# A decoder layer's second-half row norm: ScalarE normalises, weight and bias go onto the transposed banks, GpSimd makes the residual rows

## Chip, cores and metric

The kernel runs on one core of one Trainium2 chip. The metric is the device time of one execution in microseconds (us). Timed runs are given by their median; beside them stands one execution under the profiler, whose trace shows where the time goes.

## What is computed

One layer of a decoder with 1024 tokens and 1024 channels, float32 throughout. A mixer (a convolution group and a sliding-window attention group, one projection in, one out) is followed by a feed-forward network with a short convolution. After each of the two there is a residual with a factor and a LayerNorm over the 1024 channels of a token:

```python
mix = hybrid_mixer(x, ...)
x = layer_norm(DEEPNORM_ALPHA * x + mix, ln1_g[l], ln1_b[l])
ffn = conv_ffn(x, w_up[l], ffn_dw_w[l], ffn_dw_b[l], w_down[l])
x = layer_norm(DEEPNORM_ALPHA * x + ffn, ln2_g[l], ln2_b[l])

def layer_norm(x, g, b):
    mu = jnp.mean(xf, axis=-1, keepdims=True)
    var = jnp.mean(jnp.square(xf - mu), axis=-1, keepdims=True)
    y = (xf - mu) * lax.rsqrt(var + LN_EPS)
    return y * g + b
```

The change concerns the first of these LayerNorms. Its result is used twice: transposed, as input of the feed-forward network, and multiplied by alpha, as the residual of the second LayerNorm.

## The kernel before

The 1024 tokens are worked through as two halves H = 0 and H = 1 of 512 tokens, each of four blocks t of 128 tokens. Every matrix product is done in three passes over high and low parts of both operands (`wh`, `wl` for weights, `xh`, `xl` for activations): ScalarE makes the high part by a cast (L231), GpSimd the low part by a subtraction (L233). Products take 24 matmuls of 128x512: 16 with `wh` (L265, L266), then 8 with `wl` (L268).

The order in which parts of the layer are issued is written out by hand in `SCRIPT`, one letter for one step of a generator: `O` is the output projection of the second half, `s` a set of sums over the first half (`first_sums`), `L` one block of the second half's norm (`second_norm`, which calls `ln1(1, ...)`), `f` a step of the feed-forward network of the first half for its first six channel blocks (`ffn`, with `up_branch`, `up` and `down`). After the script come `last_sum` and the joint stage (`joint`), which works on both halves at once with seven products in place of eight. From the program order and its own simulation of the engines, a scheduler sets the order on each engine's queue. An engine then takes its queue in order. The large products keep their program order (`chain`).

In a block of the norm, `row_stats` (L295) takes the statistics of the 128x1024 rows `a` on VectorE, GpSimd does the inverse root (L293). For both halves the setting `LNM` selects the last branch of `layer_norm_rows`: VectorE subtracts the mean and scales (L311), GpSimd multiplies by the weight row `g` (L312), VectorE adds the bias row `b` (L313). `transpose_split` then transposes the rows in two groups of four 128x128 pieces into two PSUM banks (L278), ScalarE casts each bank to the high part (L281), VectorE subtracts to make the low part (L282). ScalarE multiplies the rows by alpha (L662). For H = 1, `other_sums` goes on in the two banks: it forms the differences between the halves that the joint stage needs (L763 to L773, executed in the helpers at L747 and L750). The second half uses three single banks, `'ln1': 'TCN'`, in turn; bank T also serves `first_sums`. The rows `a` are next read when the joint stage adds its down-projection to them (L720).

The weight and bias rows are loaded once as 128x1024 tiles spread over the partitions, in `first_norm` (`norm1`), and serve both halves. Parameters that are needed as one value for each partition are loaded as rows of 128 by DMAs from ScalarE's queue (L192 to L202) and turned by three transposes (`parameters`, L203), so that `pcol` gives a column.

Of the kernel before, what the change touches and what calls it, by code (L numbers as in the profile page):

```python
# [12 lines left out]
AF = mybir.ActivationFunctionType  # L13
ALU = mybir.AluOpType

P = 128
S = 1024
D = 1024
KT = D // P
# [12 lines left out]
ALPHA = 2.0 ** 0.25  # L32
# [37 lines left out]
def hybrid_layer_kernel(  # L70
# [7 lines left out]
    nc = tc.nc  # L78
# [22 lines left out]
    def psB(shape=(P, 512), tag="T"):  # L101
        return ps.tile(list(shape), F32, name="ps" + tag, tag=tag, bufs=PS[tag])
# [3 lines left out]
    def psk(key, shape=(P, 512)):  # L106
        tags = PT[key]
        k = ps_turn[key] = ps_turn.get(key, -1) + 1
        return psB(shape, tags[k % len(tags)])

    def f(ap):
        return ap.bitcast(F32)
# [27 lines left out]
    def ring(tag, w, n):  # L140
        if tag not in rings:
            rings[tag] = [top[0], 0, n]
            top[0] += w * n
        r = rings[tag]
        o = r[0] + r[1] % r[2] * w
        r[1] += 1
        return tiny[:, o:o + w]
# [6 lines left out]
    def early(o, n, parts=P):  # L154
        return at(56 * 4 * UNIT + 4 * (HC + o), [P, n], F32, "early")[0:parts, :]
# [3 lines left out]
    ident = const[:, 0:P]  # L159
# [16 lines left out]
    def r128(ap):  # L176
        return ap.rearrange("(r c) -> r c", c=P)
# [3 lines left out]
    pr3 = early(3 * P, P)  # L181
# [18 lines left out]
    nc.scalar.dma_start(out=pr1[34:78, :], in_=r128(ffn_dw_b))  # L200
    nc.scalar.dma_start(out=pr1[78:122, :], in_=r128(ffn_dw_w[2]))
    nc.scalar.dma_start(out=pr3[0:88, :], in_=ffn_dw_w[0:2].rearrange("k (r c) -> (k r) c", c=P))  # L202
    def parameters():  # L203
        tp = psB()
        for i, pr in enumerate((pr1, pr2, pr3)):
            nc.tensor.transpose(out=tp[:, i * P:(i + 1) * P], in_=pr, identity=ident)
        nc.vector.tensor_copy(out=par, in_=tp[:, 0:3 * P].rearrange("p (i c) -> p i c", c=P))
        nc.vector.tensor_scalar(out=bq8, in0=par[:, 0, 0:4], scalar1=-0.125, scalar2=None, op0=ALU.mult)

    def pcol(t, i):  # L210
        return par[:, t, i:i + 1]
# [8 lines left out]
    fdb = [pcol(0, 34 + i) for i in range(2 * NC)]  # L220
    fw = [[pcol(2, i) for i in range(2 * NC)], [pcol(2, 44 + i) for i in range(2 * NC)],
          [pcol(0, 78 + i) for i in range(2 * NC)]]

    def cdw(k, c):
        return pcol(1, k * 4 + c)
# [45 lines left out]
    def transpose_split(src, xh, xl, t, key):  # L271
        banks = []
        for q in range(2):
            b = psk(key)
            banks.append(b)
            for k in range(4):
                kt = q * 4 + k
                nc.tensor.transpose(out=b[:, k * P:(k + 1) * P], in_=src[:, kt * P:(kt + 1) * P], identity=ident)  # L278
            bv_ = b.rearrange("p (k t) -> p k t", t=P)
            hd = xh[q][:, :, t * P:(t + 1) * P]  # L280
            nc.scalar.copy(out=hd, in_=bv_)  # L281
            nc.vector.tensor_tensor(out=xl[q][:, :, t * P:(t + 1) * P], in0=bv_, in1=f(hd), op=ALU.subtract)  # L282
        return banks
# [6 lines left out]
    def rsqrt_eps(out_, in_, n, tag="rv"):  # L290
        v = ring(tag, 4, 4)
        nc.vector.tensor_scalar(out=v[:, 0:n], in0=in_, scalar1=EPS, scalar2=None, op0=ALU.add)  # L292
        nc.gpsimd.tensor_tensor(out=out_, in0=v[:, 0:n], in1=mhalf[:, 0:n], op=ALU.pow)  # L293

    def row_stats(r):  # L295
        st = ring("st", 12, 2).rearrange("p (a b) -> p a b", a=2)
        for i in range(2):
            nc.vector.bn_stats(out=st[:, i, :], in_=r[:, i * 512:(i + 1) * 512])
        mv = ring("mv", 2, 2)
        nc.vector.bn_aggr(out=mv, in_=st.rearrange("p a b -> p (a b)"))  # L300
        rstd = ring("rstd", 1, 2)
        rsqrt_eps(rstd, mv[:, 1:2], 1)
        return mv, rstd

    def layer_norm_rows(r, g, b, H):
        mv, rstd = row_stats(r)
        if LNM[H]:
            nc.vector.scalar_tensor_tensor(out=r, in0=r, scalar=mv[:, 0:1], in1=g, op0=ALU.subtract, op1=ALU.mult)
            nc.vector.scalar_tensor_tensor(out=r, in0=r, scalar=rstd, in1=b, op0=ALU.mult, op1=ALU.add)
        else:  # L310
            nc.vector.tensor_scalar(out=r, in0=r, scalar1=mv[:, 0:1], scalar2=rstd, op0=ALU.subtract, op1=ALU.mult)  # L311
            nc.gpsimd.tensor_tensor(out=r, in0=r, in1=g, op=ALU.mult)  # L312
            nc.vector.tensor_tensor(out=r, in0=r, in1=b, op=ALU.add)  # L313
# [12 lines left out]
    def pair(i):  # L326
        return area(2 * i), area(2 * i + 1)
# [326 lines left out]
    def ln1(H, g, b):  # L654
        (h0, l0), (h1, l1) = [pair(i) for i in ((2, 3) if H == 0 else (4, 6))]
        xh, xl = (h0, h1), (l0, l1)
        x1T[H] = (xh, xl)
        for t in range(TB):
            a = acc[H * TB + t]
            layer_norm_rows(a, g, b, H)  # L660
            banks = transpose_split(a, xh, xl, t, "ln%d" % H)
            nc.scalar.mul(out=a, in_=a, mul=ALPHA)  # L662
            if H == 1:
                other_sums(t, *[b.rearrange("p (k t) -> p k t", t=P) for b in banks])
            yield
# [97 lines left out]
    def other_sums(t, b0, b1):  # L763
        (h0, h1), (l0, l1) = [[f(part(a, t)) for a in x_] for x_ in x1T[0]]
        into(b0, b0, h0, ALU.subtract)
        into(b0, b0, l0, ALU.subtract)
        split_to(*[part(a, t) for a in pair(area_of[3])], b0)
        into(b0, h1, b0, ALU.subtract)
        into(b0, b0, l1, ALU.add)
        s2h, s2l = [part(a, t) for a in pair(area_of[2])]  # L770
        split_to(s2h, s2l, b0)
        into(b1, b1, f(s2h), ALU.subtract)
        into(part(last_f, t), b1, f(s2l), ALU.subtract)  # L773
# [207 lines left out]
    norm1 = []  # L981

    def first_norm():
        norm1.extend((bcast_row(ln1_g, 'g1'), bcast_row(ln1_b, 'b1')))
        yield from ln1(0, *norm1)
# [11 lines left out]

    def second_norm():
        lanes.update(LANES_JOINT)
        yield from ln1(1, *norm1)  # L1000

    steps = {'0': glus(0), 'h': line_bias(), 'j': once(lambda: proj_kv(0)), 'i': proj_q(0), 'x': load_x(1),
             'c': conv(0), 'a': attn(0), 'n': conv_norm(0), 'g': glus(1), 'k': once(lambda: proj_kv(1)),
             'q': proj_q(1), 'A': attn(1), 'o': out_proj(0), 'l': first_norm(), 'C': conv(1),
             'N': second_conv_norm(), 'f': ffn(0, alone), 'O': second_out(), 'L': second_norm(),
             's': first_sums()}
    drain(load_x(0))
    parameters()
    for k in SCRIPT:
        if k == 'c':  # L1010
# [63 lines left out]
```

## Time and profile before

| | us |
|---|---|
| median of 3 timed runs | 1112.17 (1111.09 to 1112.24) |
| the profiled execution | 1113.39 |
| its span, first to last instruction | 1111.6 |

| engine | busy us in the span |
|---|---|
| PE (TensorE matmul) | 1050.4 |
| DVE (VectorE) | 788.9 |
| POOL (GpSimd) | 654.5 |
| ACT (ScalarE) | 481.9 |

PE busy is not PE at its peak: matmuls are pipelined, and a row's duration is longer than the step to the next. In steady work a 128x512 matmul starts 0.23 us after the one before it. A row of the trace names the line, the engine, the operation, what is written and read (`out<-in`), shapes and counts. In groups, "busy us, mean ns" are followed by the idle time of the engine just before them and by what ended it. In a row of waits, the three numbers are the total in us, how often, and the longest. In a row of windows, the first numbers are the stretch and its length, then busy time with the number of instructions for PE, PEld (the weight loads), DVE, ACT and POOL, then the granted TensorE clock as a share of full speed, the share of the DMA engines and GB/s.

### The profile page before, as it was taken

The numbers are of one execution on the slowest core, as the hardware profiler recorded it, in microseconds if no ns is written. First come the engines' busy times: TensorE is split into PE (matmuls) and PEld (weight loads), VectorE is DVE, ScalarE is ACT, GpSimd is POOL, SyncE is SP. The second block draws the span as 40 slices with busy tenths as digits, with TensorE's granted clock in tenths as the row PEclk, the third lists the DMA queues.
The fourth block names the chain that finished last, engine by engine and source line by source line (L and its number), as shares of the span: only waits on it lengthen the run. The fifth ranks groups of instructions, "written<-read, shape, count | busy, mean of one in ns | idle before, by whom it ended". The sixth has DMA issues, their size and how long they took to land.

```text
span 1111.6 us, 14383 instructions
## 1 busy us (share of the span) xinstructions
PE 1050.4 (94%) x5113; PEld 873.9 (79%) x5113; DVE 788.9 (71%) x1430; ACT 481.9 (43%) x915; POOL 654.5 (59%) x560
## 2 busy tenths in 40 slices
PE   7999999878968999898999999999999999999996
PEld 5887778778957998676788787878788787888875
DVE  2899789999897448985746656564747566569656
ACT  4546677753548333462515242433425142442430
POOL 3749688775587556455736372746556363636551
PEclk9999999999978999899999999999999999999999
DMA  6535221413600242131211021111212110233321
GB/s 183 160 87 132 77 57 40 139 53 98 186 20 1 78 132 65 50 110 43 76 37 59 20 82 32 58 56 38 76 39 76 35 60 20 76 114 115 113 95 75
DMA packets 115641, 85.19 MB, mean 77 GB/s; under 512 B 20354, under 2 KB 108017, under 8 KB 115569
## 3 DMA queue, kind: packets, MB, share of 16 engines
q1 hardware_dynamic: 112368, 78.92, 23.9%
q10 hardware_dynamic: 3201, 5.35, 1.4%
q8 instruction: 40, 0.66, 0.2%
q14 instruction: 32, 0.26, 0.1%
HBM read 80.05 MB, written 4.21 MB: 76 GB/s over the span
## 4 chain that ended last, share of the span: by engine, by line
PE 76%; DVE 13%; DMA 4%; POOL 3%; ACT 3%; issue 1%; SPq 0%; POOLq 0%; DVEq 0%; ACTq 0%
PE psA L265 6%; PE psA L266 6%; PE psA L268 5%; PE psS L713 2%; PE psS L714 2%; PE psS L715 2%; PE psS L796 2%; PE psS L794 2%; PE psS L793 2%; PE psA L794 2%; PE psA L796 2%; PE psA L793 2%; PE psS L505 2%; PE psA L638 1%; PE psA L713 1%
## 5 line engine op out<-in xcount | busy, mean ns | idle before, releaser
L233 POOL TENSOR_TENSOR wl<-raw,wh 128x512 fp32r<-128x512 f32 x196 | 263.3, 1355 | 162.2 <-ACT wh L231 68.9
L231 ACT CAST wh<-raw 128x512 fp32r<-128x512 f32 x196 | 119.1, 620 | 173.5 <-PE psA L266 24.1
L233 POOL TENSOR_TENSOR wl<-ts,wh 128x512 fp32r<-128x512 f32 x64 | 82.5, 1296 | 155.4 <-ACT wh L231 135.5
L421 DVE SCALAR_TENSOR_TENSOR psC<-hconv,const,psC 128x512 f32<-128x512 f32 x196 | 147.3, 751 | 3.5
L265 PE MATMUL psA<-x,wh 128*128 128x512 f32 x336 | 135.9, 404 | 7.9 <-DVE z L678 4.1
L266 PE MATMUL psA<-x,wh 128*128 128x512 f32 x336 | 134.4, 400 | 0.0
L231 ACT CAST wh<-ts 128x512 fp32r<-128x512 f32 x64 | 39.3, 622 | 177.4 <-PE psS L715 39.2
L268 PE MATMUL psA<-x,wl 128*128 128x512 f32 x336 | 87.2, 396 | 0.6 <-POOL wl L233 0.6
L265 PEld LDWEIGHTS psA<-x,wh 128*128 128x128 f32 x336 | 64.9, 193 | 23.9 <-issue 4.7
L266 PEld LDWEIGHTS psA<-x,wh 128*128 128x128 f32 x336 | 64.9, 193 | 13.5 <-issue 0.2
L268 PEld LDWEIGHTS psA<-x,wl 128*128 128x128 f32 x336 | 62.3, 188 | 15.1 <-issue 1.2
L293 POOL TENSOR_TENSOR tiny<-tiny,const 128x1 f32<-128x1 f32 (+1 forms) x28 | 26.5, 951 | 53.7 <-DVE tiny L292 50.7
L720 DVE TENSOR_TENSOR acc<-psS,acc 128x512 f32<-128x512 f32 x52 | 35.7, 688 | 31.4 <-PE psS L715 31.4
L233 POOL TENSOR_TENSOR ol<-or,oh 128x512 fp32r<-128x512 f32 x32 | 40.7, 1296 | 18.9 <-ACT oh L231 16.6
L793 PE MATMUL psA<-x,wh 128*128 128x512 f32 x112 | 43.6, 389 | 0.0
L794 PE MATMUL psA<-x,wh 128*128 128x512 f32 x112 | 43.6, 389 | 0.0
L793 PE MATMUL psS<-x,wh 128*128 128x512 f32 x112 | 43.6, 389 | 0.0
L794 PE MATMUL psS<-x,wh 128*128 128x512 f32 x112 | 43.6, 389 | 0.0
L832 POOL TENSOR_TENSOR ts<-raw,ts 128x512 f32<-128x512 f32 x32 | 42.0, 1313 | 1.3
L413 POOL TENSOR_TENSOR cp<-cp,cp 128x512 f32<-128x512 f32 x28 | 36.0, 1287 | 8.4 <-ACT cp L409 8.4
L713 PE MATMUL psS<-wh,gh 128*128 128x512 f32 x88 | 35.0, 397 | 5.9 <-ACT gh L693 3.1
L638 PE MATMUL psA<-oh,x 128*128 128x256 f32 x128 | 37.9, 296 | 1.9 <-ACT z L399 1.5
(383 smaller groups left out, 3057.9 us busy)
## 6 DMA issues: line engine op xcount, KB each, us to landing
raw<-in_w_up SPq DMA_DIRECT2D x56, 512.0 KB
raw<-in_w_down SPq DMA_DIRECT2D x28, 512.0 KB
raw<-in_w_in SPq DMA_DIRECT2D x20, 512.0 KB
raw<-in_x SPq DMA_DIRECT2D x8, 512.0 KB
raw<-in_w_in SPq DMA_DIRECT2D x16, 256.0 KB
acc<-in_x SPq DMA_DIRECT2D x8, 512.0 KB
or<-in_w_out SPq DMA_DIRECT2D x64, 64.0 KB
or<-in_w_out SPq DMA_DIRECT2D x8, 512.0 KB
```

What stands on the lines that cost most here:

```text
L231: nc.scalar.copy(out=h, in_=part)
L233: nc.gpsimd.tensor_tensor(out=l, in0=part, in1=f(h), op=ALU.subtract)
L265: m.append(nc.tensor.matmul(out=o, lhsT=wh[kt], rhs=xh[kt], start=kt == 0, stop=False))
L266: m.append(nc.tensor.matmul(out=o, lhsT=wh[kt], rhs=xl[kt], start=False, stop=False))
L268: m.append(nc.tensor.matmul(out=o, lhsT=wl[kt], rhs=xh[kt], start=False, stop=kt == KT - 1))
L421: tap(nc.vector.scalar_tensor_tensor(out=dst if k == KO else total, in0=src, scalar=cdw(k, c), in1=total, op0=ALU.mult, op1=ALU.add))
L638: m.append(nc.tensor.matmul(out=pa[:, 0, :], lhsT=yah[:, c, :], rhs=wa[0][c], start=c == 0, stop=False))
L713: m.append(nc.tensor.matmul(out=o, lhsT=gh[:, tsl], rhs=wh, start=j == 0, stop=False))
L793: m.append(nc.tensor.matmul(out=o, lhsT=wh[k], rhs=xh[k], start=k == 0, stop=False))
L794: m.append(nc.tensor.matmul(out=o, lhsT=wh[k], rhs=xl[k], start=False, stop=False))
L796: m.append(nc.tensor.matmul(out=o, lhsT=wl[k], rhs=xh[k], start=False, stop=k == 3))
L832: nc.gpsimd.tensor_tensor(out=t, in0=x0, in1=x1, op=ALU.subtract)
```

## The change

In the second half, ScalarE applies mean and inverse deviation to the rows in one pass, with the inverse deviation as scale and a new column `shift` (minus mean times inverse deviation, VectorE, 128x1) as bias. The rows are transposed without weight and bias. In the two PSUM banks, ScalarE then applies weight and bias in place, for each of the four 128x128 pieces with one column of each. The copies `l1g` and `l1b` of the parameters for this come from two more DMAs of 8 rows into `pr3`. The cast, the low part and `other_sums` stay. The residual rows are made by GpSimd from the normalised rows by a multiplication and an addition with weight and bias rows that have been multiplied by alpha once (two passes of ScalarE over 128x1024), so that the pass with alpha over the rows goes. The first half is computed as before.

```diff
     nc.scalar.dma_start(out=pr3[0:88, :], in_=ffn_dw_w[0:2].rearrange("k (r c) -> (k r) c", c=P))
+    nc.scalar.dma_start(out=pr3[88:96, :], in_=r128(ln1_g))
+    nc.scalar.dma_start(out=pr3[96:104, :], in_=r128(ln1_b))
...
+    l1g = [pcol(2, 88 + i) for i in range(KT)]
+    l1b = [pcol(2, 96 + i) for i in range(KT)]
...
+    def transpose_norm(src, xh, xl, t, key):
+        banks = []
+        for q in range(2):
+            b = psk(key)
+            banks.append(b)
+            for k in range(4):
+                kt = q * 4 + k
+                nc.tensor.transpose(out=b[:, k * P:(k + 1) * P], in_=src[:, kt * P:(kt + 1) * P], identity=ident)
+            for k in range(4):
+                kt = q * 4 + k
+                col = b[:, k * P:(k + 1) * P]
+                nc.scalar.activation(out=col, in_=col, func=AF.Identity, bias=l1b[kt], scale=l1g[kt])
             bv_ = b.rearrange("p (k t) -> p k t", t=P)
             hd = xh[q][:, :, t * P:(t + 1) * P]
             nc.scalar.copy(out=hd, in_=bv_)
...
-            layer_norm_rows(a, g, b, H)
-            banks = transpose_split(a, xh, xl, t, "ln%d" % H)
-            nc.scalar.mul(out=a, in_=a, mul=ALPHA)
+            if H == 0:
+                layer_norm_rows(a, g, b, H)
+                transpose_split(a, xh, xl, t, "ln0")
+                nc.scalar.mul(out=a, in_=a, mul=ALPHA)
+            else:
+                mv, rstd = row_stats(a)
+                shift = ring("shift1", 1, 2)
+                nc.vector.scalar_tensor_tensor(out=shift, in0=mv[:, 0:1], scalar=-1.0, in1=rstd,
+                                               op0=ALU.mult, op1=ALU.mult)
+                nc.scalar.activation(out=a, in_=a, func=AF.Identity, bias=shift, scale=rstd)
+                banks = transpose_norm(a, xh, xl, t, "ln1")
+                nc.gpsimd.tensor_tensor(out=a, in0=a, in1=g, op=ALU.mult)
+                nc.gpsimd.tensor_tensor(out=a, in0=a, in1=b, op=ALU.add)
             if H == 1:
                 other_sums(t, *[b.rearrange("p (k t) -> p k t", t=P) for b in banks])
...
     def second_norm():
         lanes.update(LANES_JOINT)
+        for row in norm1:
+            nc.scalar.mul(out=row, in_=row, mul=ALPHA)
         yield from ln1(1, *norm1)
```

More of the change, by code (lines that the diff above doesn't have):

```diff
@@ L278, in transpose_split @@
                 nc.tensor.transpose(out=b[:, k * P:(k + 1) * P], in_=src[:, kt * P:(kt + 1) * P], identity=ident)
+            bv_ = b.rearrange("p (k t) -> p k t", t=P)
+            hd = xh[q][:, :, t * P:(t + 1) * P]
+            nc.scalar.copy(out=hd, in_=bv_)
+            nc.vector.tensor_tensor(out=xl[q][:, :, t * P:(t + 1) * P], in0=bv_, in1=f(hd), op=ALU.subtract)
+        return banks
+    def transpose_norm(src, xh, xl, t, key):
[10 more added lines that the diff above has]
+                nc.scalar.activation(out=col, in_=col, func=AF.Identity, bias=l1b[kt], scale=l1g[kt])
             bv_ = b.rearrange("p (k t) -> p k t", t=P)
```

## The prediction

> **What bounds the kernel now.** I read the page first, for the busy shares of the engines, then the table of windows around the changed stage, then what the matmuls waited for there, and last the rows of VectorE (DVE), ScalarE (ACT) and GpSimd (POOL) in it.
>
> ```profile
> PE 1050.4 (94%) x5113; PEld 873.9 (79%) x5113; DVE 788.9 (71%) x1430; ACT 481.9 (43%) x915; POOL 654.5 (59%) x560
> ...
> 420.00:500.00 80.00, 74.33 (x363) 61.42 (x363) 76.01 (x122) 37.03 (x63) 45.97 (x31) 0.96 0.24 71
> 510.00:1000.00 490.00, 481.15 (x2113) 395.72 (x2112) 296.62 (x498) 182.99 (x309) 265.39 (x208) 1.00 0.18 56
> ```
>
> TensorE is busy for 94% of the span, so the time can only fall where TensorE loses time. From 510 to 1000 us it loses 8.9 us in 490 (490 - 481.15), with a granted clock of 1.00: what an earlier start of that stage gains is kept to the end. The second half's norm runs between about 422 and 495 us. There VectorE is busy for 76.0 of 80 us (95%), ScalarE for 37.0 (46%) and GpSimd for 46.0 (57%). In this stage VectorE, not TensorE, is the full engine.
>
> What TensorE loses there is in the next rows: the waits of the matmuls between 410 and 520 us, then three stretches of 10 us (the last three numbers of a row are the granted clock, the DMA share and GB/s).
>
> ```profile
> PE psA L265 <- DVE z L678: 4.1, 2, 3.5
> PE psS L713 <- ACT gh L693: 3.1, 1, 3.1
> PE psA L265 <- ACT wh L231: 0.7, 1, 0.7
> PE psA L268 <- POOL wl L233: 0.6, 1, 0.6
> PE psS L715 <- DVE gl L694: 0.2, 1, 0.2
> ...
> 450.00:460.00 10.00, 6.26 (x26) 4.59 (x25) 10.00 (x12) 5.69 (x10) 7.20 (x4) 0.90 0.36 105
> 460.00:470.00 10.00, 10.00 (x40) 8.06 (x39) 9.61 (x18) 3.67 (x7) 0.00 (x0) 0.76 0.01 2
> 500.00:510.00 10.00, 6.88 (x23) 5.16 (x22) 6.83 (x10) 2.64 (x5) 5.86 (x4) 0.83 0.07 20
> ```
>
> The waits sum to 8.7 us (4.1 + 3.1 + 0.7 + 0.6 + 0.2). After each of the two long ones the clock drops: 0.76 in the ten microseconds after the wait of 3.5 us, which costs 0.24 x 10 = 2.4 us, and 0.83 around the wait of 3.1 us, which costs 0.17 x 10 = 1.7 us. So the stage loses 12.8 us in all, and this is the most that the change can win here. The first stall, 3.5 + 2.4 = 5.9 us, ends with VectorE's L678, the last step of the up-projection's convolution. The second, 3.1 + 1.7 = 4.8 us, ends with ScalarE's L693.
>
> **What VectorE no longer does.** The next rows are the groups of VectorE and GpSimd in the stage, and single rows of the time line.
>
> ```profile
> L313 DVE TENSOR_TENSOR acc<-acc,bo 128x1024 f32<-128x1024 f32 x4 | 6.3, 1581 | 0.0
> L311 DVE TENSOR_SCALAR acc<-acc,tiny 128x1024 f32<-128x1024 f32 x4 | 5.0, 1272 | 0.0
> L691 DVE TENSOR_TENSOR z<-z,z 128x512 f32<-128x512 f32 x3 | 4.3, 1450 | 0.1
> L694 DVE TENSOR_TENSOR gl<-z,gh 128x512 fp32r<-128x512 f32 x4 | 4.1, 1020 | 0.7 <-ACT gh L693 0.7
> L691 DVE TENSOR_TENSOR z<-z,sq 128x512 f32<-128x512 f32 x1 | 1.6, 1582 | 0.0
> L292 DVE TENSOR_SCALAR tiny<-tiny 128x1 f32<-128x1 f32 x4 | 0.6, 146 | 0.0
> L312 POOL TENSOR_TENSOR acc<-acc,g 128x1024 f32<-128x1024 f32 x4 | 10.4, 2600 | 2.4 <-DVE acc L311 2.4
> ...
> 447.37 2.53 DVE L691 TENSOR_TENSOR z<-z,z 128x512 f32<-128x512 f32 x1
> 449.82 2.31 DVE L313 TENSOR_TENSOR acc<-acc,bo 128x1024 f32<-128x1024 f32 x1
> 452.05 1.78 DVE L694 TENSOR_TENSOR gl<-z,gh 128x512 fp32r<-128x512 f32 x1
> 458.39 0.73 DVE L678 SCALAR_TENSOR_TENSOR z<-psA,const,z 128x510 f32<-128x510 f32 x1
> 464.61 0.68 DVE L691 TENSOR_TENSOR z<-z,z 128x512 f32<-128x512 f32 x1
> 444.17 5.18 POOL L312 TENSOR_TENSOR acc<-acc,g 128x1024 f32<-128x1024 f32 x2
> ```
>
> Removed: four L311 (5.0 us) and four L313 (6.3 us), 11.3 us of VectorE's time. All eight lie ahead of the L678 at 458.39 that ends the first stall. Added: four `shift` operations on 128x1; the nearest row is L292 with 0.146 us, so 0.6 us at most.
>
> The same rows show that VectorE and GpSimd hinder one another. L691 takes 0.68 us alone (464.61, where the window row has GpSimd at 0.00) and 2.53 us at 447.37, beside the two L312 that end at 449.35. The four L691 and four L694 together take 4.3 + 1.6 + 4.1 = 10.0 us in place of 8 x 0.68 = 5.4, an excess of 4.6 us at a GpSimd share of 57%. The change doubles the row operations on GpSimd: eight of 2.60 us in place of four, 10.4 us more, a share of 70% (56.4 of 80). By proportion the excess grows to 4.6 x 70/57 = 5.6 us, so 1.0 more. The bounds are zero, if the new operations fall where VectorE has no operation on two SBUF inputs, and 8 x 2.60 = 20.8, if each holds one up for its whole length. I take 1.0. VectorE's balance is 11.3 - 0.6 - 1.0 = 9.7 us.
>
> The Trainium skill says in "SBUF — State Buffer", "Who interferes with whom", that a VectorE instruction with two SBUF inputs and a GpSimd instruction that reads SBUF exclude one another, and that the one which starts first holds the shared pair for its whole length. The 2.53 us of L691 agree. By that rule the doubled GpSimd work speaks against the change, and it is a rival below.
>
> **What this relief is worth.** L678 at 458.39 is late only because the queue ahead of it is full; with 9.7 us less in that queue, more than the 3.5 us that TensorE waited, the first stall should go with its slow clock: 5.9 us. The second stall is another case. It is the tail behind the last row block: ScalarE's casts of the last sum stand in its queue ahead of the last up-projection's bias (L673), and TensorE has nothing left in order but what needs L693.
>
> ```profile
> 497.99 1.65 ACT L750 CAST x<-lastf 128x512 fp32r<-128x512 f32 x3
> 499.55 0.78 ACT L673 ACTIVATE z<-psA,const 128x512 f32<-128x512 f32 x1
> 504.17 0.62 ACT L693 CAST gh<-z 128x512 fp32r<-128x512 f32 x1 [2.66 <-DVE z L691]
> ```
>
> An earlier start moves these three together, so I leave the 4.8 us in, and I leave the 1.5 us of short waits.
>
> **What ScalarE takes over.** The rows are the groups of the scale that goes, of the bank's cast, of the bias with two column operands, and a four-way scaling of 128x128 out of PSUM from the attention.
>
> ```profile
> L662 ACT ACTIVATE acc<-acc 128x1024 f32<-128x1024 f32 x4 | 4.3, 1068 | 0.0
> L281 ACT CAST x<-psC 128x512 fp32r<-128x512 f32 x3 | 1.8, 589 | 0.3 <-PE psC L278 0.3
> L673 ACT ACTIVATE z<-psA,const 128x512 f32<-128x512 f32 x7 | 5.5, 779 | 2.8 <-PE psA L268 2.8
> ...
> L565 ACT ACTIVATE x<-psY,const x32: 345/367/387, 159.8 to 369.8; 128x128 fp32r<-128x128 f32 x32
> ```
>
> Two column operands cost 779 - 589 = 190 ns over a plain pass. The row norm is then L662 plus that, 1.26 us, and it takes the place of L662 (1.07): four times 0.19 = 0.8 us more. Thirty-two operations on 128x128 go into the banks: 0.37 each by L565, which has one column operand, 0.46 with half of the 190 ns on top; I take 0.37, so 11.8 us (14.7 at the upper end). No row shows one of them writing PSUM in place; below, the start-to-start step of L565 would be less than its 0.37, and I allow 0.29, so 9.3. Scaling the two rows of weight and bias by alpha is two of L662, 2.1 us. In all 14.7 us more, 51.7 of 80: ScalarE still has room. It lies beside TensorE, except that a bank is held 4 x 0.37 = 1.5 us longer before its cast. Against this stands the path ahead of the transposes: L311, L312 and L313 (1.27 + 2.60 + 1.58 = 5.5 us) are replaced by a shift and one ScalarE pass (0.15 + 1.26 = 1.4), so a block is 4.1 us earlier before its two banks cost it up to 3.0. I count this pair at nothing; if the transposes do not move up, the cost of the bank steps is open, up to 4 x 3.0 = 12 us.
>
> **What GpSimd takes over.** The multiply moves behind the transposes and an add follows it: a pair of 2 x 2.60 = 5.2 us per block. The rows that it makes are first needed in the joint stage, long after. But its queue is in order, and the low halves of the weights (L233) stand in it, for which the last eight of the 24 matmuls of an up-projection wait.
>
> ```profile
> L233 POOL TENSOR_TENSOR wl<-raw,wh 128x512 fp32r<-128x512 f32 x23 | 34.2, 1513 | 30.5 <-PE psS L714 16.2 <-PE psA L268 6.1 <-PE psY L715 4.5
> ...
> 495.15 1.81 PE psA L268 x8
> ```
>
> Sixteen matmuls run first, 2 x 1.81 = 3.6 us of cover. One pair ahead of a needed split costs 5.2 - 3.6 = 1.6 us; GpSimd's idle 30.5 us around these splits hides most pairs. I count one: 1.6 us.
>
> **The start.** Two more DMAs of 8 rows are issued from ScalarE's queue.
>
> ```profile
> 12.09 0.30 ACTq L202 DMA_DIRECT2D early<-in_ffn_dw_w  x1
> 12.84 0.58 ACT L281 CAST x<-psT 128x512 fp32r<-128x512 f32 x1 [0.52 <-DMA early<-in_ffn_dw_w]
> 14.98 0.62 ACT L231 CAST wh<-raw 128x512 fp32r<-128x512 f32 x1 [1.56 <-DMA raw<-in_w_in]
> ```
>
> At 0.30 us each they delay the cast at 12.84 by 0.6, and the 1.56 us of idle before the next ScalarE work hide that. Without this cover it costs 0.6 us.
>
> **The sum.** -5.9 + 1.6 = -4.3 us. The profiled execution took 1113.39 us (span 1111.6), 1.22 above the median of the three timed runs, 1112.17. On the profiled execution's scale that is 1109.1, on the median's 1107.9, and I forecast the latter.
>
> **The rivals.** *Both stalls go.* If the last block's transposes come up by more than the 4.1 us, the last sum is done before L673 needs ScalarE, and nearly all of the 12.8 us goes: 1112.17 - 11 = 1101. For it speaks VectorE's 95%, against it the in-order tail above. *GpSimd holds VectorE up.* If each of the eight row operations meets one two-input operation of VectorE and holds it for half its length, that is 8 x 1.3 = 10.4 us against the 11.3 removed; the first stall stays and the time is 1112. The Trainium skill's rule named above ("SBUF — State Buffer") is this mechanism. *The banks take the place of the rows.* The three PSUM banks of this norm are reused by the four blocks; with 1.5 us more per bank on three uses in turn, 4.5 us cancel the 4.3, and the time is 1112 again. *Slower: GpSimd becomes the gate.* If the pairs of two blocks stand together ahead of a needed split, TensorE waits 10.4 - 3.6 = 6.8 us and pays a slow clock of 2.4 behind it: +9.2 against -5.9, so 1115.5, and up to 1118 where a single pair also lands badly. It decides from the point at which over 5.9 + 3.6 = 9.5 us of row work is ahead of one split. For it speaks that GpSimd, with 70%, becomes the second fullest engine; against it, its idle stretch from 457 to 473 us. *The change moves other work.* The order on each engine is made by a scheduler that simulates the whole program, so that the two DMAs and the new operations can reorder work elsewhere, or the pass be placed so late that nothing is relieved. The short waits in the stage (0.6 and 0.7 us) say what a few such shifts cost: within 3 us either way.
>
> **How the numbers follow.** Chances: forecast 0.40 (1103 to 1109.9); both stalls go 0.12; GpSimd holds VectorE up 0.08; the banks 0.11; GpSimd as the gate 0.21; other work moved 0.08, of which 0.02 faster, 0.02 same, 0.04 slower. About 0.2%, 2.2 us, is what a measurement of this kernel can tell from no change. Faster is 0.40 + 0.12 + 0.02 = 0.54, same 0.08 + 0.11 + 0.02 = 0.21, slower 0.21 + 0.04 = 0.25. The range goes from 1100 (most of the 12.8 us) to 1117 (the slower rival without its worst end). The forecast's own range is 1103 to 1109.9.
>
> **What would show it.** Right: the wait of L265 for L678 is gone and the clock at 460 to 470 us is near 1.00, VectorE has about 10 us less in the stage, and the joint stage's first product starts 4 to 5 us earlier. Wrong: L691 and L694 with a mean above 1.4 us (GpSimd holds VectorE), waits of L268 for L233 of several microseconds (GpSimd as the gate), waits of the transposes or of ScalarE's bank steps that end late (the banks), or a difference that stands already before 420 us (other work moved).

## The result and the profile after

| | before | after |
|---|---|---|
| median of 4 timed runs, us | 1112.2 (1111.09 to 1112.52) | 1106.2 (1104.47 to 1107.02) |
| the profiled execution, us | 1113.39 | 1105.66 |
| its span, us | 1111.6 | 1103.9 |

The four of before are the three timed runs shown above and one more. The ratio on record is 0.9939, with a 95% interval of 0.9922 to 0.9956; the two medians alone divide to 0.9946, which lies inside it. They differ by 6.0 us, where 4.3 were forecast. The profile of after is read in the same order as that of before. Lines of the code have moved: the matmuls of the large products are now L270, L271 and L273, ScalarE's cast of the weights L236, GpSimd's low part L238, the up-projection's bias L706, its convolution's last step L711, `gh` L726, `gl` L727, and the down-projection L746 to L748. First the page's busy times of the engines:

```profile
PE 1047.1 (95%) x5113; PEld 872.3 (79%) x5113; DVE 780.9 (71%) x1426; ACT 496.3 (45%) x949; POOL 660.6 (60%) x564
```

Over the whole span VectorE has 8.0 us less (788.9 before), ScalarE 14.4 more (481.9) and GpSimd 6.1 more (654.5). Next the windows view of after, over the stretches that were shown of before (busy times of PE, PEld, DVE, ACT and POOL, then granted clock, DMA share, GB/s):

```profile
420.00:500.00 80.00, 73.54 (x359) 60.76 (x359) 68.90 (x120) 51.59 (x97) 54.94 (x37) 0.99 0.24 73
450.00:460.00 10.00, 9.35 (x46) 7.47 (x45) 9.96 (x17) 5.92 (x14) 4.15 (x3) 1.00 0.20 58
460.00:470.00 10.00, 8.87 (x40) 6.80 (x39) 9.41 (x17) 6.41 (x13) 8.82 (x5) 1.00 0.18 54
490.00:500.00 10.00, 6.73 (x27) 5.19 (x26) 7.35 (x9) 4.80 (x9) 7.15 (x6) 0.93 0.18 52
500.00:510.00 10.00, 10.00 (x42) 8.14 (x41) 4.87 (x8) 1.78 (x3) 3.10 (x3) 0.90 0.00 0
```

The clock between 450 and 470 us is 1.00, where it was 0.90 and 0.76. It still falls around 500 us (0.93, then 0.90). What the matmuls of after waited for between 410 and 520 us (total, how often, longest) says why:

```profile
PE psS L746 <- ACT gh L726: 3.9, 2, 3.3
PE psA L270 <- ACT wh L236: 1.4, 1, 1.4
PE psA L273 <- POOL wl L238: 0.8, 1, 0.8
PE psS L829 <- POOL wl L238: 0.5, 1, 0.5
PE psS L748 <- DVE gl L727: 0.3, 1, 0.3
```

The first stall, the wait for the up-projection's convolution, is gone from the list. The second, for `gh`, stands there with 3.3 us. The wait of 0.5 us at L829 belongs to the joint stage (it ends at 513.34). Before has the same one at its own L796, 0.5 us, but at 520.68 and so just outside its list. Without it the rows of after sum to 6.4 us, against 8.7 before: the waits give 2.3. The 4.1 us for the convolution are gone, and longer waits for `gh` (0.8 more), `wh` (0.7), `wl` (0.2) and `gl` (0.1) have taken 1.8 back. The rest is the clock, in one window over the stage, first of before and then of after:

```profile
420.00:510.00 90.00, 81.20 (x384) 66.57 (x384) 82.84 (x131) 39.66 (x67) 51.83 (x35) 0.94 0.22 66
```

```profile
420.00:510.00 90.00, 83.54 (x399) 68.90 (x399) 73.77 (x128) 53.37 (x100) 58.04 (x40) 0.98 0.22 65
```

A clock of 0.98 in place of 0.94 over 90 us is 3.6 us. With the 2.3 us of waits that makes 5.9. This is an estimate: a clock rounded to hundredths leaves each of the two open by 0.45 us. To compare runs, a stage with ends of its own serves better than fixed times: from the last matmul of the second half's output projection to the first product of the joint stage's down-projection into bank A. These two marks are the last and the first start time in two rows of the trace by line, here for before and then for after:

```profile
L644 PE MATMUL psA<-oh,x x128: 278/283/283, 223.5 to 428.8; 128*128 128x256 f32 x128
L713 PE MATMUL psA<-wh,gh x64: 387/389/496, 553.0 to 1008.3; 128*128 128x512 f32 x64
```

```profile
L667 PE MATMUL psA<-oh,x x128: 277/283/283, 221.0 to 426.6; 128*128 128x256 f32 x128
L746 PE MATMUL psA<-wh,gh x64: 389/389/496, 545.7 to 1000.5; 128*128 128x512 f32 x64
```

The stage takes 553.0 - 428.8 = 124.2 us before and 545.7 - 426.6 = 119.1 after: 5.1 less. Of the 7.7 us between the two spans, 2.2 stood already at the stage's start (428.8 and 426.6), and the joint stage gives the last 0.5 (455.3 us from first to last product, then 454.8). The 2.2 us go back to the first 25 us, before anything of this change but its two DMAs: the first product into bank S starts at 24.1 us in before and at 21.5 in after. In the time line, the products ahead of it follow at steps of 0.43 us in before (16.24, 16.67) and of 0.24 us in after (15.90, 16.14): TensorE's slow steps at the start last longer in the one execution than in the other. Whether the change does this is asked below (e4 and e5).

### The profile page after: what moved, and what is told of

Same layout as the page of the kernel before. It is cut to its first block, busy times and chain, and to the rows that moved or that the text cites. A ratio compares the mean times of both kernels' runs of the same rounds, so it can differ in the third digit from the quotient of the medians.

```text
span 1103.9 us, 14411 instructions
## 1 busy us (share of the span) xinstructions
PE 1047.1 (95%) x5113; PEld 872.3 (79%) x5113; DVE 780.9 (71%) x1426; ACT 496.3 (45%) x949; POOL 660.6 (60%) x564
## 4 chain that ended last, share of the span: by engine, by line
PE 77%; DVE 11%; POOL 4%; DMA 3%; ACT 3%; issue 1%; SPq 0%; POOLq 0%; ACTq 0%; DVEq 0%
PE psA L270 6%; PE psA L271 6%; PE psA L273 6%; PE psS L746 2%; PE psS L748 2%; PE psS L747 2%; PE psS L829 2%; PE psA L829 2%; PE psA L827 2%; PE psS L827 2%; PE psA L826 2%; PE psS L826 2%; PE psS L528 2%; DVE psC L444 1%; PE psA L661 1%
## 5 line engine op out<-in xcount | busy, mean ns | idle before, releaser
L238 POOL TENSOR_TENSOR wl<-raw,wh 128x512 fp32r<-128x512 f32 x196 | 260.1, 1339 | 139.0 <-ACT wh L236 67.4
L236 ACT CAST wh<-raw 128x512 fp32r<-128x512 f32 x196 | 119.2, 619 | 168.3 <-PE psA L271 19.9
L238 POOL TENSOR_TENSOR wl<-ts,wh 128x512 fp32r<-128x512 f32 x64 | 82.5, 1296 | 155.1 <-ACT wh L236 135.3
L270 PE MATMUL psA<-x,wh 128*128 128x512 f32 x336 | 132.7, 395 | 4.4 <-ACT wh L236 3.5
L271 PE MATMUL psA<-x,wh 128*128 128x512 f32 x336 | 132.0, 393 | 1.4 <-DVE x L287 1.4
L236 ACT CAST wh<-ts 128x512 fp32r<-128x512 f32 x64 | 39.4, 622 | 177.4 <-PE psS L748 39.2
L273 PE MATMUL psA<-x,wl 128*128 128x512 f32 x336 | 87.2, 395 | 0.8 <-POOL wl L238 0.8
L270 PEld LDWEIGHTS psA<-x,wh 128*128 128x128 f32 x336 | 63.1, 188 | 19.1 <-ACT wh L236 4.1
L271 PEld LDWEIGHTS psA<-x,wh 128*128 128x128 f32 x336 | 63.1, 188 | 14.6 <-DVE x L287 1.7
L273 PEld LDWEIGHTS psA<-x,wl 128*128 128x128 f32 x336 | 62.4, 188 | 15.3 <-POOL wl L238 1.2
L238 POOL TENSOR_TENSOR ol<-or,oh 128x512 fp32r<-128x512 f32 x32 | 40.7, 1292 | 17.3 <-ACT oh L236 17.3
L826 PE MATMUL psA<-x,wh 128*128 128x512 f32 x112 | 43.6, 389 | 0.0
L827 PE MATMUL psA<-x,wh 128*128 128x512 f32 x112 | 43.6, 389 | 0.0
L865 POOL TENSOR_TENSOR ts<-raw,ts 128x512 f32<-128x512 f32 x32 | 41.9, 1310 | 1.3
L746 PE MATMUL psS<-wh,gh 128*128 128x512 f32 x88 | 34.9, 397 | 6.3 <-ACT gh L726 3.9
```

The lines of the kernel that those rows point to most:

```text
L236: nc.scalar.copy(out=h, in_=part)
L238: nc.gpsimd.tensor_tensor(out=l, in0=part, in1=f(h), op=ALU.subtract)
L270: m.append(nc.tensor.matmul(out=o, lhsT=wh[kt], rhs=xh[kt], start=kt == 0, stop=False))
L271: m.append(nc.tensor.matmul(out=o, lhsT=wh[kt], rhs=xl[kt], start=False, stop=False))
L273: m.append(nc.tensor.matmul(out=o, lhsT=wl[kt], rhs=xh[kt], start=False, stop=kt == KT - 1))
L746: m.append(nc.tensor.matmul(out=o, lhsT=gh[:, tsl], rhs=wh, start=j == 0, stop=False))
```

## Experiments

All of them are read by the same stage. The table has its length, VectorE's busy time in it from the windows view, the median of the timed runs, and the ratio to before of the same set with its 95% interval.

| run | stage, us | DVE busy, us | median, us | ratio |
|---|---|---|---|---|
| before | 124.2 | 99.4 | | |
| after | 119.1 | 89.6 | 1106.2 | 0.9939 [0.9922, 0.9956] |
| e1, rows on VectorE | 125.4 | 97.2 | 1114.47 | 1.0015 [0.9999, 1.0032] |
| e2, norm on VectorE | 118.8 | 90.5 | 1108.88 | 0.9972 [0.9958, 0.9986] |
| e3, ScalarE norm alone | 123.3 | 99.0 | 1112.32 | 1.0004 [0.9991, 1.0016] |
| e4, two DMAs alone | 123.8 | 100.3 | 1112.03 | 1.0013 [0.9995, 1.0031] |
| e5, after again | 118.9 | 89.3 | 1107.47 | 0.9952 [0.9935, 0.9970] |
| e6, last casts on VectorE | 122.1 | 92.7 | 1109.77 | 0.9969 [0.9953, 0.9985] |
| e7, bank steps out | 119.9 | 88.9 | 1108.37 | 0.9958 [0.9939, 0.9977] |
| e8, row steps out | 120.4 | 87.0 | 1109.93 | 0.9969 [0.9952, 0.9986] |
| e9, tail in order | 116.4 | 89.8 | 1102.64 | 0.9904 [0.9878, 0.9930] |
| e10, row steps halved | 120.3 | 87.6 | 1108.01 | 0.9958 [0.9940, 0.9976] |
| e11, e9 again | 114.2 | 88.3 | 1102.99 | 0.9915 [0.9895, 0.9935] |
| e12, e9 and e10 | 115.4 | 86.0 | 1104.07 | 0.9927 [0.9903, 0.9950] |

One program twice gives the noise of a single trace: after and e5 differ by 0.2 us in the stage, e9 and e11 by 2.2. Differences of a stage length below about 2 us decide nothing here.

### Is it VectorE's relief, or the shorter path?

The theory of the prediction (A in the expectations) is that VectorE's queue was full and has less in it now. Its rival (B) is that the path from the statistics to the transposes is shorter. The windows of VectorE ahead of the first stall speak for A. Here are the stretches from 430 to 450 us of before, then of after:

```profile
430.00:440.00 10.00, 10.00 (x47) 8.23 (x46) 10.00 (x20) 3.93 (x7) 7.52 (x7) 1.00 0.14 52
440.00:450.00 10.00, 9.35 (x48) 7.67 (x47) 9.96 (x11) 3.25 (x7) 10.00 (x7) 1.00 0.18 52
```

```profile
430.00:440.00 10.00, 10.00 (x52) 8.38 (x51) 6.40 (x17) 9.70 (x17) 6.24 (x6) 1.00 0.15 53
440.00:450.00 10.00, 10.00 (x46) 8.28 (x45) 9.28 (x12) 7.47 (x16) 8.82 (x6) 1.00 0.36 100
```

In before VectorE is busy for 10.00, 9.96 and 10.00 us of the three stretches from 430 to 460, so it did not stand waiting for rows or banks ahead of the late L678 at 458.39. In after it has 6.40 and 9.28 in the first two, and the L711 in its place starts at 450.04.

e1 keeps the path of after and puts the row operations on VectorE, behind the transposes:

```diff
-                nc.gpsimd.tensor_tensor(out=a, in0=a, in1=g, op=ALU.mult)
-                nc.gpsimd.tensor_tensor(out=a, in0=a, in1=b, op=ALU.add)
+                nc.vector.tensor_tensor(out=a, in0=a, in1=g, op=ALU.mult)
+                nc.vector.tensor_tensor(out=a, in0=a, in1=b, op=ALU.add)
```

> As the changed kernel, but the residual rows are made by VectorE (two 128x1024 operations per block, 4 x 2 x about 1.2 us = 9.6 us) and not by GpSimd. Theory A (the gain is VectorE's relief): the 9.7 us are taken back, the first stall returns, 1109 to 1113 us. Rival B (the gain is the shorter path ahead of the transposes, whatever VectorE carries): the path is the same as in the changed kernel, 1105 to 1107 us. Rival C (the gain comes from the start, by the two new DMAs): 1105 to 1107 as well.

The groups of e1 (busy us, mean ns, then idle time before them) have the 12.0 us that went back:

```profile
L694 DVE TENSOR_TENSOR acc<-acc,g 128x1024 f32<-128x1024 f32 x4 | 6.0, 1503 | 3.0 <-PE psT L297 3.0
L695 DVE TENSOR_TENSOR acc<-acc,bo 128x1024 f32<-128x1024 f32 x4 | 6.0, 1492 | 0.0
```

The whole gain is gone: a stage of 125.4 us and a ratio of 1.0015, although mean, deviation, weight and bias are still applied by ScalarE, as in after. The median of 1114.47 lies just above A's range and far above B's. A had expected the first stall itself to return, and it did not: no product into bank A waits for the convolution, and the clock from 460 to 470 us is 1.00. Only two of the eight row operations stand ahead of that step (L711 at 453.10). The loss comes later, where the other six are. These are waits of e1 between 410 and 520 us that neither before nor after has:

```profile
PE psT L297 <- issue: 2.3, 1, 2.3
PE psY L746 <- DVE z L711: 1.7, 1, 1.7
PE psY L746 <- DVE acc L753: 1.1, 1, 1.1
```

Two of them end with VectorE by name. The first has no releaser in the profile; its transposes into bank T start at 472.41, 0.1 us after VectorE's last read of that bank (L780, 471.64 to 472.31), so VectorE is its likely cause. The cleanest pair is e1 and e8 (below), which has no row operations on any engine: with the path of after in both, VectorE's 12.0 us lengthen the stage from 120.4 to 125.4 us, and the intervals of the two ratios are apart. So the short path alone gives nothing when VectorE is full, which is A against B. That the relief would do without the shorter path is not shown; e3 was meant to test it.

e2 puts one part back, the row norm, as a single operation of VectorE in place of the shift and of ScalarE's pass. GpSimd keeps both row operations.

```diff
-                shift = ring("shift1", 1, 2)
-                nc.vector.scalar_tensor_tensor(out=shift, in0=mv[:, 0:1], scalar=-1.0, in1=rstd, ...)
-                nc.scalar.activation(out=a, in_=a, func=AF.Identity, bias=shift, scale=rstd)
+                nc.vector.tensor_scalar(out=a, in0=a, scalar1=mv[:, 0:1], scalar2=rstd, op0=ALU.subtract, op1=ALU.mult)
```

> As the changed kernel, but the row norm is VectorE's tensor_scalar of before (L311) in place of shift and ScalarE's pass. Theory A: VectorE gets back 4 x 0.8 to 1.25 us = 3.2 to 5.0 of the 9.7 it was relieved of; what is left, 5 to 6 us, still covers the wait of 3.5, so 1106 to 1109. Rival B: the path ahead of the transposes stays short (no L312, no L313), 1105 to 1107. If ScalarE's pass is what counts: 1110 to 1113.

The stage is 118.8 us: it holds the whole gain without ScalarE's row norm, the step that the change's title begins with. The median of 1108.88 lies in A's range. In the groups of e2 that operation costs less than it did before, 3.2 us for four (5.0 before):

```profile
L689 DVE TENSOR_SCALAR acc<-acc,tiny 128x1024 f32<-128x1024 f32 x4 | 3.2, 802 | 0.0
```

VectorE's total is only 0.9 us above that of after, for its eight two-input operations of the up-projection take 7.9 us here (11.1 in after). What relieves VectorE enough is thus the bias row, which went to GpSimd, together with an order that lets the norm run faster. The timed ratio of e2 is the weaker of the two (0.9972, after 0.9939 and 0.9952). Its profile is 0.9 us longer than that of e5 behind the stage (a span of 1106.8 less 548.1, where e5 has 1105.8 less 548.0). Where that comes from stays open.

e3 is the other half: ScalarE normalises, and all else is as before, with the bias row on VectorE ahead of the transposes and no work in the banks.

```diff
                 nc.scalar.activation(out=a, in_=a, func=AF.Identity, bias=shift, scale=rstd)
-                banks = transpose_norm(a, xh, xl, t, "ln1")
                 nc.gpsimd.tensor_tensor(out=a, in0=a, in1=g, op=ALU.mult)
-                nc.gpsimd.tensor_tensor(out=a, in0=a, in1=b, op=ALU.add)
+                nc.vector.tensor_tensor(out=a, in0=a, in1=b, op=ALU.add)
+                banks = transpose_split(a, xh, xl, t, "ln1")
+                nc.scalar.mul(out=a, in_=a, mul=ALPHA)
...
-        for row in norm1:
-            nc.scalar.mul(out=row, in_=row, mul=ALPHA)
```

> As the changed kernel in the row norm (ScalarE), but weight and bias on the rows ahead of the transposes as before (GpSimd multiplies, VectorE adds), the banks as before, ScalarE's pass with alpha back. Theory A: VectorE is relieved of 5.0 - 0.6 = 4.4 us, just over the wait of 3.5, so part of the gain, 1107 to 1110. Rival B: the path still holds L312 and L313 and gains nothing, 1111 to 1113.

No gain (1.0004), though 5.0 us of L311 were to go for 0.6 us of shifts. The windows row says that VectorE was not relieved at all (99.0 us, before 99.4), and the groups of e3 say why:

```profile
L694 DVE TENSOR_TENSOR acc<-acc,bo 128x1024 f32<-128x1024 f32 x4 | 7.4, 1852 | 0.0
L690 DVE SCALAR_TENSOR_TENSOR tiny<-tiny 128x1 f32<-128x1 f32 x4 | 3.9, 973 | 0.4 <-POOL tiny L316 0.4
```

7.4 + 3.9 = 11.3 us, by chance just the 5.0 + 6.3 that the two operations of before took. The shift works on one number for each partition, and its four take 0.97 us in the mean. The time line of e3 shows the longest of them inside an operation of GpSimd:

```profile
440.70 3.15 POOL L693 TENSOR_TENSOR acc<-acc,g 128x1024 f32<-128x1024 f32 x1
441.51 2.36 DVE L690 SCALAR_TENSOR_TENSOR tiny<-tiny 128x1 f32<-128x1 f32 x1
```

Both end at about 443.86 us. An operation planned at 0.15 us took as long as the rest of the GpSimd operation beside it. In after, where the row operations of GpSimd follow the transposes, all four shifts run alone (the trace of after by line: shortest, median and longest in ns):

```profile
L690 DVE SCALAR_TENSOR_TENSOR tiny<-tiny x4: 149/154/160, 425.0 to 434.9; 128x1 f32<-128x1 f32 x4
```

So A's forecast of 1107 to 1110 failed because the relief failed, and B's of 1111 to 1113 came true. e3 fits A's count as measured (no relief, no gain), but it can't tell A from B: it has neither the relief nor the short path.

### What the added work costs

e4 is before with the two DMAs of the start alone, and e5 is after once more.

```diff
+    nc.scalar.dma_start(out=pr3[88:96, :], in_=r128(ln1_g))
+    nc.scalar.dma_start(out=pr3[96:104, :], in_=r128(ln1_b))
```

> The kernel before with the two DMAs of 8 rows and nothing else (the columns are not used). Theories A and B: no change, 1111 to 1113 us. Rival C (the 2.5 us by which the changed kernel's profile is ahead at 24 us come from the DMAs at the start): 1109 to 1110, with the first products at the full clock in its profile.

> The changed kernel once more, as the measure for the other runs of this set. 1105 to 1108 us. Its first profile had its first products at the full clock and was 2.5 us ahead at 24 us; if that is the phase of the clock and not the change, this profile may begin slow and be ahead by about 5 us only, all of it between 428 and 500 us.

e4 doesn't move the time (1.0013 [0.9995, 1.0031]). In e5 the same program as after starts its first product into bank S at 23.1 us, not at 21.5, and keeps the stage of 118.9. Its stage starts at 429.1 us, where that of before starts at 428.8. So the DMAs give and cost nothing that can be measured, and the 2.2 us by which the profile of after is ahead at the stage belong to the execution.

e7 and e8 leave out one added cost each: the thirty-two steps of ScalarE in the banks, and the eight row operations of GpSimd.

```diff
-            for k in range(4):
-                kt = q * 4 + k
-                col = b[:, k * P:(k + 1) * P]
-                nc.scalar.activation(out=col, in_=col, func=AF.Identity, bias=l1b[kt], scale=l1g[kt])
```

> The changed kernel without the 32 operations that apply weight and bias in the banks; the feed-forward input of the second half lacks weight and bias. If these 14 us of ScalarE lie beside other work and their delay of the banks is paid by the shorter path, as the prediction counts: within 1 us of the changed kernel. If the banks are what is late now: 2 to 5 us faster.

```diff
-                nc.gpsimd.tensor_tensor(out=a, in0=a, in1=g, op=ALU.mult)
-                nc.gpsimd.tensor_tensor(out=a, in0=a, in1=b, op=ALU.add)
```

> The changed kernel without the eight row operations on GpSimd; the residual rows of the second half lack weight, bias and alpha. The prediction's price for them is 1.6 us (GpSimd's queue) plus some of the 1.0 us by which VectorE is held up: 1.5 to 3 us faster than the changed kernel. If GpSimd is the gate now: 4 us or more. If they are hidden: no change within 1 us.

Neither is faster than e5 of the same set (1108.37 and 1109.93 against 1107.47). e8 was expected within 1 us or faster and came out 2.5 us slower, though its interval overlaps that of e5. So no cost of either can be measured. The price of 1.6 us for GpSimd's queue isn't there: the longest wait for the low parts is 0.6 us in e8 and 0.8 in after. But leaving out work also changes the order, and what e8 saves there it loses at ScalarE's cast of the weights, for which one wait is 2.5 us long (1.4 in after).

### What ends the second stall

The prediction put the second stall down to ScalarE's queue: the casts of the last sum stand ahead of the last up-projection's bias. e6 moves those casts to VectorE.

```diff
-            split_to(*[x_[k] for x_ in sums[4]], last_f[:, k, :])
+            h, l = [x_[k] for x_ in sums[4]]
+            nc.vector.tensor_copy(out=h, in_=last_f[:, k, :])
+            into(l, last_f[:, k, :], f(h), ALU.subtract)
```

> The changed kernel, with the four casts of the last sum (the high parts in last_sum) on VectorE and not on ScalarE. If the second stall is ScalarE's queue ahead of the last up-projection's bias, as the prediction says: the bias comes up to 2.2 us earlier (the four casts take 2.17 us in the changed kernel) and the time is 1.5 to 3 us under the changed kernel's. Rival (VectorE's queue ends the stall): no change within 1 us.

Neither came true: the time is 2.3 us above that of e5, and the stall got longer. In the waits of e6 between 410 and 520 us it is 4.8 us,

```profile
PE psS L746 <- ACT gh L726: 5.4, 2, 4.8
```

and its time line shows what the convolution stood behind:

```profile
494.22 1.53 DVE L813 CAST x<-lastf 128x512 fp32r<-128x512 f32 x3
...
496.60 1.88 DVE L780 TENSOR_TENSOR x<-lastf,x 128x512 fp32r<-128x512 f32 x3
498.48 0.73 DVE L709 SCALAR_TENSOR_TENSOR z<-psA,const,z 128x511 f32<-128x511 f32 x1
```

L709 is a step of the last up-projection's convolution, and it starts where the last sum's work on VectorE ends. The time line of after has the last sum ahead on both engines, so that clearing one queue could not do:

```profile
489.64 2.17 ACT L783 CAST x<-lastf 128x512 fp32r<-128x512 f32 x4
490.28 3.36 DVE L780 TENSOR_TENSOR x<-lastf,x 128x512 fp32r<-128x512 f32 x4 [1.27 <-ACT x L783]
491.71 0.77 ACT L706 ACTIVATE z<-psA,const 128x512 f32<-128x512 f32 x1
493.63 0.73 DVE L709 SCALAR_TENSOR_TENSOR z<-psA,const,z 128x511 f32<-128x511 f32 x1
...
496.85 0.62 ACT L726 CAST gh<-z 128x512 fp32r<-128x512 f32 x1 [2.80 <-DVE z L724]
```

L706 starts when the casts are done, and L709 waits 1.15 us more (492.48 to 493.63) for the subtractions. e9 therefore orders both, the casts behind the last up-projection's `gh` and the subtractions behind its `gl`. Nothing else of after changes.

```diff
+            up_end[0] = (nc.scalar.copy(out=gh, in_=zu),
+                         nc.vector.tensor_tensor(out=gl, in0=zu, in1=f(gh), op=ALU.subtract))
...
+            i = nc.scalar.copy(out=h, in_=last_f[:, k, :])
+            j = nc.vector.tensor_tensor(out=l, in0=last_f[:, k, :], in1=f(h), op=ALU.subtract)
+            for o, before in zip((i, j), up_end[0]):
+                tc.add_manual_dep(o.ins, before.ins.name, order, reason="the last up-projection first")
```

> The changed kernel, with the casts and subtractions of the last sum ordered behind the last up-projection's gate (its gh on ScalarE, its gl on VectorE). In the run with the casts on VectorE the last L709 stood behind them there, so the second stall is taken to end with both queues. If so, gh comes about 3 us earlier, the stall of 3.3 us and its slow clock of 1.7 go, and the time is 2 to 4 us under the changed kernel's. Rival (the joint stage's second product needs the last sum's buffers, by way of GpSimd's ts, and waits as long): no change within 1 us, the wait only moves to the products.

> The kernel with the last sum behind the last up-projection, once more: its first set had six runs only. If the second stall was worth what its profile shows (2.7 us between the second half's output projection and the first joint down-projection), 1103 to 1106 us, a ratio of 0.991 to 0.995; if the first set's 0.9904 was in part the phase of the clock at the start, the upper end of that.

The time line of e9 has the casts of the last sum (now L815) behind `gh` (L728):

```profile
494.82 0.62 ACT L728 CAST gh<-z 128x512 fp32r<-128x512 f32 x1 [2.45 <-DVE z L726]
495.34 2.18 ACT L815 CAST x<-lastf 128x512 fp32r<-128x512 f32 x4
```

Measured from the start of the stage, `gh` comes 1.8 us earlier than in after (68.42 us in place of 70.25), not 3. About half of it is the queue of VectorE: L709 starts at 66.1 in place of 67.0. The other half is the product of the two branches ahead of `gh` (`z<-z,sq`), which takes 0.69 us in place of 1.58: in after GpSimd's L865 runs beside it, which needs the last sum and now comes later.

The longest wait for `gh` goes from 3.3 to 1.2 us in e9 and to 0.6 in e11, whose longest waits between 410 and 520 us are these (the one at L832, for ScalarE's cast of the weights, is new):

```profile
PE psA L270 <- ACT wh L236: 1.4, 1, 1.4
PE psT L832 <- ACT wh L236: 0.9, 1, 0.9
PE psA L273 <- POOL wl L238: 0.8, 1, 0.8
PE psS L748 <- ACT gh L728: 0.6, 1, 0.6
```

The windows row of e11 over its stage has a clock of 1.00:

```profile
429.00:543.20 114.20, 110.14 (x497) 90.01 (x496) 88.25 (x148) 68.21 (x127) 84.70 (x61) 1.00 0.24 74
```

At 1102.64 and 1102.99 us, with ratios of 0.9904 and 0.9915, this version beats both kernels: some 4 us on top of the change, against the 5.0 that the prediction's count gives for the second stall in after (3.3 and a slow clock of 1.7). After and e9 were timed in different sets, and the ends of their intervals touch (0.9922 to 0.9956 and 0.9878 to 0.9930). Within e9's own set, e10, which is after with halved row steps and has after's tail, is 5.4 us slower than e9, and these intervals are apart.

### Shorter operations on GpSimd

The last question is the contention: do half as long operations on GpSimd hinder VectorE less, and does that shorten the stage? e10 halves them, and e12 is e10 with the order of e9.

```diff
-                nc.gpsimd.tensor_tensor(out=a, in0=a, in1=g, op=ALU.mult)
-                nc.gpsimd.tensor_tensor(out=a, in0=a, in1=b, op=ALU.add)
+                for c in (slice(0, 512), slice(512, D)):
+                    nc.gpsimd.tensor_tensor(out=a[:, c], in0=a[:, c], in1=g[:, c], op=ALU.mult)
+                    nc.gpsimd.tensor_tensor(out=a[:, c], in0=a[:, c], in1=b[:, c], op=ALU.add)
```

> The changed kernel, with each of the eight row operations on GpSimd split in two of 128x512. If VectorE's operations on two SBUF inputs wait for the end of the GpSimd operation that runs, the excess of L724 and L727 (11.1 - 5.4 = 5.7 us in the changed kernel) falls to 3 to 4.5 us. The time falls by at most 1 us if VectorE still sets the stage; no change within 1 us if, as without the row operations, something else ends it.

> The same order of the last sum, with the row operations on GpSimd in halves as well. In its own run the halving took the excess of L724 and L727 from 5.6 to 2.3 us and gained nothing, so: within 1 us of the kernel with the order alone. If VectorE sets the stage again now that the tail is shorter: 1 to 3 us faster than it.

These are VectorE's two-input operations of the up-projection in the stage, first the groups of after, then those of e10:

```profile
L727 DVE TENSOR_TENSOR gl<-z,gh 128x512 fp32r<-128x512 f32 x4 | 5.6, 1404 | 1.4 <-ACT gh L726 1.4
L724 DVE TENSOR_TENSOR z<-z,z 128x512 f32<-128x512 f32 x3 | 3.9, 1294 | 0.0
L724 DVE TENSOR_TENSOR z<-z,sq 128x512 f32<-128x512 f32 x1 | 1.6, 1581 | 0.0
```

```profile
L728 DVE TENSOR_TENSOR gl<-z,gh 128x512 fp32r<-128x512 f32 x4 | 3.4, 840 | 1.4 <-ACT gh L727 1.4
L725 DVE TENSOR_TENSOR z<-z,z 128x512 f32<-128x512 f32 x3 | 2.7, 910 | 0.0
L725 DVE TENSOR_TENSOR z<-z,sq 128x512 f32<-128x512 f32 x1 | 1.6, 1575 | 0.0
```

11.1 us become 7.7. Above the 5.4 that eight of them take alone, 5.7 us of excess become 2.3, less than the 3 to 4.5 that were expected. Of the 2.3, 0.9 are `z<-z,sq`, which runs beside GpSimd's work for the last sum and not beside a row operation; e8, without row operations, has an excess of 1.3. The time doesn't follow: 1108.01 for e10 and 1104.07 for e12, neither below its partner without the halving (1106.2 and 1107.47, 1102.64 and 1102.99). One reason is seen in the waits: in e10 and e12 those of the products for the weights' low parts (`PE psA L273 <- POOL wl L238`) sum to 2.6 us, where after and e11 have 0.8, so the halves also stand differently in GpSimd's queue. e10 alone doesn't show, then, that more relief of VectorE is worth nothing. With e8, where VectorE has 2.6 us less than in after and ScalarE's cast of the weights is late instead, it shows that a further 2 to 3 us of relief were not turned into time, because other engines were late next.

## Why the prediction held, step by step

**VectorE's balance** was forecast at 9.7 us and measured at 9.8 (99.4 to 89.6 in the stage). So close a match is luck: e4 and e5, the other profiles of the two orders, give 11.0. Its parts held too: the shifts take 0.15 us each, and L724 and L727 take 11.1 us where their forerunners took 10.0, so the contention grew by 1.1 where 1.0 was forecast (their mean is 1.38 us; that of L727 alone, 1404 ns, just passes the 1.4 that was named as a sign of the rival, without the rival's loss). That the share of GpSimd sets this number isn't shown: with as many row operations on GpSimd, e2 has 7.9 us and e10 7.7. And it depends on the order: in e3, with a row operation of GpSimd ahead of the transposes, the same four shifts cost 3.9 us.

**The first stall** went with its slow clock, as forecast at 5.9 us: its wait is gone, and with it a shorter one of 0.6 us for the same step that the forecast had not counted; the clock at 460 to 470 us is 1.00 in place of 0.76. That VectorE's full queue made it is read from the trace of before, where VectorE has no gap ahead of L678. e1 shows that VectorE's load costs the same amount again, in other waits. The clock's 2.4 us are the figure of one profile: e4 has the same wait of 3.5 us with 0.85 behind it, and e3 has waits of 2.3 and 3.2 us before 470 us with 1.00 throughout.

**The second stall** stayed, as forecast. The reason given, ScalarE's queue, was half of it: the last sum's subtractions stand on VectorE ahead of the convolution of the same block. e6, built on the half reason, made the stall longer. e9, built on both, cut it from 3.3 to 1.2 us, and to 0.6 in e11.

**ScalarE's work** was 14.0 us in the banks and 1.24 us for a pass, hidden as forecast. A bank step took 0.44 us, between the 0.37 that was taken and its upper bound of 0.46:

```profile
L301 ACT ACTIVATE psC<-psC,const 128x128 f32<-128x128 f32 x12 | 5.3, 439 | 0.2
L692 ACT ACTIVATE acc<-acc,tiny 128x1024 f32<-128x1024 f32 x4 | 5.0, 1244 | 2.6 <-DVE tiny L690 2.6
```

These are groups of after; the steps in banks T and N take 5.2 and 3.5 us. The rival of the banks would need waits of the transposes or of these steps that end late. Among the waits of the matmuls of after none is for a bank, and e7, without the steps, isn't faster.

**GpSimd's pairs** are the term that was mis-sized. The 1.6 us for one pair ahead of a needed split were not found: the matmuls' wait for the low parts is 0.8 us where it was 0.6, so 0.2, and e8, without the pairs, isn't faster. The eight operations themselves take 9.6 + 10.3 = 19.9 us (20.8 forecast), in the groups of after:

```profile
L695 POOL TENSOR_TENSOR acc<-acc,bo 128x1024 f32<-128x1024 f32 x4 | 10.3, 2568 | 0.2
L694 POOL TENSOR_TENSOR acc<-acc,g 128x1024 f32<-128x1024 f32 x4 | 9.6, 2398 | 5.8 <-PE psT L297 5.8
```

The rival of GpSimd as the gate had its price worked out from two pairs that stand together. The longest such stretch in after is three row operations, from 457.73 to 465.29 us, ahead of the split that ends the wait of 0.8 us. That is 7.6 us, under the 9.5 from which this rival was to decide.

**The sum** was -4.3 us, and the stage gave -5.1 (e5: -5.3). Without the 1.6 us of GpSimd the forecast would have been -5.9. Waits that were not in it took back nearly the same: 0.8 us more for `gh`, 0.7 for ScalarE's cast of the weights (1.4 where 0.7 stood) and 0.1 for `gl`. That they make up for the mis-sized term is luck. The timed medians of after and e5 are 6.0 and 5.5 us under those of before in their own sets. One named sign of being wrong, a difference ahead of 420 us, stood in the profile of after with 2.2 us; e5 shows that the execution made it and not the change.

## What to carry to other kernels

Count an engine's relief in measured rows: a tiny operation of VectorE with two inputs in SBUF can cost what GpSimd does beside it, and not what its own size suggests (e3). When a stall ends in the tail of a chain, look at every queue that the chain passes: moving the obstacle from one of them to another lengthened the stall here (e6), and ordering it behind the chain on both cut it (e9, e11). Once the full engine has slack, look for what is late next: here further relief of VectorE was met by waits for the weights' high parts (e8) and low parts (e10).

## What was not expected of the hardware

A VectorE operation of 128x1 took 150 ns alone and 2358 ns beside a 128x1024 operation of GpSimd. The Trainium skill says in "SBUF — State Buffer", "Who interferes with whom", that a VectorE instruction with two SBUF inputs contends with a GpSimd instruction that reads SBUF, and that the port pair they share is an exclusive lock. The 2358 ns agree with it, for the shift has two inputs in SBUF.

The length of the slow steps at the start differs between executions of one program: the first product into bank S starts at 21.5 us in after and at 23.1 in e5, and at 21.5 in e9 and 22.9 in e11. Two profiles of one program can so differ by 1.6 us that no edit made; the stage's own length is counted from a later mark.
